# A two-layer decoder trunk on one core: staging slots and a PSUM sum for the first two modulation vectors

## The chip, the cores and the metric

One Trainium2 chip, of which the kernel uses one core. The metric is the device time of one execution in microseconds (us). Three runs of the kernel before gave 2352.1 to 2356.06 us, with a median of 2353.39 us. The engines are called as in the profile: PE (TensorE matmul) and PEld (its weight loads), DVE (VectorE), ACT (ScalarE), POOL (GpSimd), SP (the engine that issues nearly all transfers).

## What is computed

Layer 0 is sparse attention, layer 1 a short gated convolution; each is followed by a SwiGLU FFN. Each of the four sub-layers is normed and modulated by six vectors per layer that come from the condition c. The change touches only the front of layer 0: the first norm and the vectors sh1 (j = 0) and sc1 (j = 1).

```python
c_act = jax.nn.silu(c)                              # c: (1, 1024)
for i in range(2):
    mod = c_act @ ada_w[i] + ada_b[i]               # ada_w: (2, 1024, 6144)
    sh1, sc1, g1, sh2, sc2, g2 = split(mod, 6)      # j = 0 .. 5
    h = _rmsnorm(x, norm1_g[i]) * (1.0 + sc1) + sh1 # x: (1, 1024, 1024)
    y = _dsa_mixer(h, ...) if i == 0 else _short_conv_mixer(h, ...)
    x = x + g1 * y
    h = _rmsnorm(x, norm2_g[i]) * (1.0 + sc2) + sh2
    x = x + g2 * _swiglu(h, ...)
```

All is float32; a large product runs as three products of rounded high and low parts (`hi`, `lo`).

## The kernel before

A planner in the kernel (`Plan`) records every operation with an engine, an estimated cost and a priority (`plan.pri`, smaller is sooner). `drain` then emits the instructions in the order in which its own model of the engines would start them; each engine runs its list strictly in that order. Every instruction therefore carries line 244 (the emitter), and the rows are told apart by their tiles. A change at the front shifts the model's times, so it can also change the order much later.

The front is `Attention.first_norm` (line 851). x arrives as eight tiles `xs` of 128 tokens by 1024 (four in the slot `lo0`, four in `lo1`). PE transposes each in eight 128x128 pieces into two PSUM banks `ps_mm`, ACT copies four pieces at a time to `xt`, and ACT squares the tile with a running sum (`junk`, `ss`). After four tiles a small chain on DVE and ACT (`rst`, with a square root) gives `nr`; PE spreads it over the partitions (`ps_L`), and DVE multiplies it into `zs`, eight tiles of 128x512 for each half of the tokens.

For the modulation vectors the loop `for j in (1, 0)` loads 1024 rows of `ada_w` in eight tiles of 128x1024 (512 KB). Per tile (a step, k = 0 to 7) DVE multiplies columns 0 to 639 by the condition `cact` and adds them to `sc` (`ada_step`, 128x640), and PE multiplies the last 384 columns with `cact` in three matmuls that have one column each (`ada_pe`, 128x1; the profile counts each twice). In the kernel before every step of `ada_pe` takes a `ps_mm` bank, and DVE adds its three columns to `mod` (128x3). At the end PE sums `sc` over the partitions by matmuls with `ones` (`ps_sm`, five of one column), DVE adds this to `mod` (128x5), and for j = 1 `ada_scale` makes `aff`. Slots: odd k take the tile `stage`, k = 0 and 4 the ring `raw` (two slots), k = 2 and 6 the ring `s4` (three).

When `aff` and `mod` of j = 0 are there, DVE and ACT form `nz` (normed and modulated, 128x512, eight for each half), ACT rounds it to `hhi`, DVE takes the rest as `hlo`, and PE begins with the product of 72 columns for the indexer (`ps_mm<-hhi,whi 128*72`), 24 matmuls for each half of the tokens; called the first product here.

`vectors` (line 614) loads the norm gains, convolution weights and small tables as rows, and DVE copies two of them (`COPY C<-S`), before PE transposes all to `vec`. `setup` (line 585) does this for c and the biases, with the Silu that gives `cact`.

Of the kernel before, what the change touches and what calls it, by code (L numbers as in the profile page):

```python
# [9 lines left out]
F32 = mybir.dt.float32  # L10
# [5 lines left out]
ALU = mybir.AluOpType  # L16
# [459 lines left out]
R_C, R_N1, R_N2, R_CW, R_G, R_IF = 0, 8, 24, 40, (64, 96), 66  # L476
# [10 lines left out]
class Trunk:  # L487
# [94 lines left out]
        nc.vector.tensor_tensor(out, r, t, op=ALU.mult)  # L582


    def setup(self, c, ada_b, arenas):
        nc, cp = self.nc, self.cp
        self.ident = ident = cp.tile([P, P], F32, name="ident")
        nc.gpsimd.memset(ident, 1.0)
        nc.gpsimd.affine_select(ident, ident, pattern=[[-1, P]], compare_op=ALU.is_equal,
                                fill=0.0, base=0, channel_multiplier=1)  # L590
        self.ones = cp.tile([P, 1], F32, name="ones")
        nc.vector.memset(self.ones, 1.0)
        self.blk4 = cp.tile([P, 4], F32, name="blk4")
        nc.vector.memset(self.blk4, 0.0)
        for i in range(4):
            nc.vector.memset(self.blk4[32 * i:32 * i + 32, i:i + 1], 1.0)
        rc, rowb = arenas[0].part_of(0)[0:8, P:2 * P], arenas[1].part_of(0)[0:96, 0:P]
        nc.sync.dma_start(rc, c.rearrange("o (k p) -> (o k) p", p=P))
        self.plan.pri = 1.2
        nc.sync.dma_start(rowb, ada_b.rearrange("l (k p) -> (l k) p", p=P))  # L600
        self.cact = cp.tile([P, 8], F32, name="cact")
        pv = self.ps("sm")
        nc.tensor.transpose(pv[:, 0:8], rc, ident[:8, :8])
        nc.scalar.activation(self.cact, pv[:, 0:8], AF.Silu)
        self.adab = cp.tile([P, 96], F32, name="adab")
        pb = self.ps("sm")
        nc.tensor.transpose(pb[:, 0:96], rowb, ident[:96, :96])
        nc.vector.tensor_copy(self.adab, pb[:, 0:96])
        mod = cp.tile([P, 2, 6, 8], F32, name="mod")
        self.mod = [[mod.part_of((i, j))[:, i, j] for j in range(6)] for i in range(2)]  # L610
        aff = cp.tile([P, 2, 2, 8], F32, name="aff")
        self.aff = [[aff.part_of((i, j))[:, i, j] for j in range(2)] for i in range(2)]

    def vectors(self, n1, n2, conv_w, gq, gk, lg, lb, rope_c, arenas, kgb):

        nc, cp = self.nc, self.cp
        rows = arenas[0].part_of(1)[:, 0:P]
        nc.vector.memset(rows, 0.0)
        for r0, n, v in ((R_N1, 16, n1.rearrange("l (k p) -> (l k) p", p=P)),
                         (R_N2, 16, n2.rearrange("l (k p) -> (l k) p", p=P)),  # L620
                         (R_CW, 24, conv_w.rearrange("o w (k p) -> (o w k) p", p=P)),
                         (R_IF, 1, rope_c)):
            nc.sync.dma_start(rows.part_of((1, r0))[r0:r0 + n, :], v)
        g = arenas[1].part_of(96)[96:98, 0:HD]
        for r, v in enumerate((gq, gk)):
            nc.sync.dma_start(g[r:r + 1], v)
        self.plan.pri = 1.15
        for i, r in enumerate(R_G):
            nc.vector.tensor_copy(
                rows.part_of((1, r))[r:r + 2].rearrange("p (r q) -> p r q", q=32),  # L630
                g[:, 32 * i:32 * i + 32].unsqueeze(1).to_broadcast([2, 4, 32]))
        self.vec = vec = cp.tile([P, P], F32, name="vec")
        pv = self.ps("sm")
        rd = [1] + [(1, r) for r in (R_N1, R_N2, R_CW, R_IF, *R_G)]
        nc.tensor.transpose(pv[:, 0:P], rows.part_of(rd), self.ident)
        nc.vector.tensor_copy(vec, pv[:, 0:P])
        self.plan.pri = 25.5
# [31 lines left out]
        if j in (1, 4) and c0 + n == KT or layer == 0 and j == 1:  # L669
            self.ada_scale(layer, j)  # L670

    def ada_pe(self, w, layer, j, k, d0, tag="mm"):


        n = w.free // P
        ps, dst, b0 = self.ps(tag), self.mod[layer][j][:, d0:d0 + n], layer * 48 + j * 8 + d0
        for d in range(n):
            self.nc.tensor.matmul(ps[:, d:d + 1], w[:, blk(d)], self.cact[:, k:k + 1],
                                  start=True, stop=True)
        self.nc.vector.tensor_tensor(dst, ps[:, 0:n], dst if k else self.adab[:, b0:b0 + n],  # L680
                                     op=ALU.add)

    def ada_scale(self, layer, j):

        n, r0 = (0, R_N1) if j == 1 else (1, R_N2)
        r0 += 8 * layer
        self.nc.vector.scalar_tensor_tensor(self.aff[layer][n], self.mod[layer][j], 1.0,
                                            self.vec[:, r0:r0 + 8], op0=ALU.add, op1=ALU.mult)
# [79 lines left out]
def trunk_kernel(tc, x, c, positions, ada_w, ada_b, norm1_g, norm2_g, attn_w_in, attn_q_norm_g,  # L768
                 attn_k_norm_g, idx_k_ln_g, idx_k_ln_b, attn_w_out, conv_w_in, conv_w,
                 conv_w_out, ffn_w_gate, ffn_w_up, ffn_w_down, rope_c, out):  # L770
    plan = Plan(tc.nc, tc)
    with ExitStack() as ctx:
        ctx.enter_context(tc.manual_schedule())
        tk = Trunk(plan)
        for p in (tk.cp, tk.pp):
# [32 lines left out]
class Attention:  # L808
# [42 lines left out]
    def first_norm(self, x, positions, setup, vectors):  # L851
        tk, nc, plan, sp = self.tk, self.nc, self.plan, self.pj
# [8 lines left out]
        for tt in range(TB):  # L861
# [40 lines left out]
        for half in range(NH):
            z, tags = [], ("rt", "t2", "sw", "rt", "t2", "sw", "rt", "rt")
            for d in range(KT):
# [3 lines left out]
                a, b = tk.aff[0][0][:, d:d + 1], tk.mod[0][0][:, d:d + 1]  # L908
# [929 lines left out]
```

## Time and profile before

| | before |
|---|---|
| median of three runs | 2353.39 us |
| the profiled execution's own time | 2353.95 us |
| its span | 2352.2 us |
| PE busy | 2263.6 us (96%) |
| DVE busy | 1887.3 us (80%) |
| ACT busy | 1121.7 us (48%) |
| DMA, mean over the span | 132 GB/s |

The profiled execution's time is its span and 1.75 us around it, and it lies 0.56 us above the median. Busy times are shares of the whole span; the change is made in its first 75 us, so the stretch itself has to be read. Digits in the slices are tenths; `PEclk` is the clock that PE was granted, in tenths of 2.4 GHz.

### The profile page before, as it was taken

Reading aid. Unit: us, or ns where it says so; the run is one execution under the profiler, and the core shown is the slowest. Engines: PE = TensorE matmul, PEld = TensorE weight load, DVE = VectorE, ACT = ScalarE, POOL = GpSimd, SP = SyncE. Lnnn points to the kernel's source line nnn. Section 1 sums busy time; section 2 is a strip of 40 time slices with the busy share of each in tenths; the row PEclk is TensorE's granted clock in tenths of the full one; section 3 lists DMA queues with packets and bytes.
Section 4 is the critical chain, followed back from the end, with each engine's and each line's share of the span. In section 5 each row is a group of like instructions: output and inputs, shape, how many; then the busy total and the mean of one; then the engine's idle time right before and its main releaser. Section 6 shows DMA issues by size and latency. Waiting matters only on the chain.

```text
span 2352.2 us, 32869 instructions
## 1 busy us (share of the span) xinstructions
PE 2263.6 (96%) x11743; PEld 1828.6 (78%) x11743; DVE 1887.3 (80%) x3858; ACT 1121.7 (48%) x2106; POOL 5.1 (0%) x19
## 2 busy tenths in 40 slices
PE   7999989999999999999999899999999999999999
PEld 6757866776797778888887677788878888888877
DVE  5789979686589888887699989886898766665996
ACT  4468989857754233333343552223553333333434
POOL 0000000000000000000000000000000000000000
PEclk7999999999999999999999999999999999999999
DMA  7414332322244756443944143334344222238343
GB/s 287 123 53 99 102 105 73 117 91 64 81 140 131 223 177 188 151 153 111 326 139 147 63 131 113 103 90 152 109 126 152 89 90 76 90 119 311 126 161 112
DMA packets 304078, 311.27 MB, mean 132 GB/s; under 512 B 15113, under 2 KB 208682, under 8 KB 303914
## 3 DMA queue, kind: packets, MB, share of 16 engines
q1 hardware_dynamic: 302474, 307.86, 41.1%
q8 instruction: 92, 1.51, 0.3%
q10 hardware_dynamic: 1440, 1.31, 0.2%
q14 instruction: 72, 0.59, 0.1%
HBM read 258.00 MB, written 51.12 MB: 131 GB/s over the span
## 4 chain that ended last, share of the span: by engine, by line
PE 74%; DVE 16%; DMA 6%; ACT 2%; issue 2%; SPq 0%; ACTq 0%; DVEq 0%
PE ps_g L244 38%; PE ps_mm L244 26%; PE ps_sm L244 5%; DVE u L244 2%; PE ps_L L244 2%; PE ps_o L244 2%; DVE wlo L244 2%; DVE sc L244 2%; DMA adaw<-in_ada_w_dram 2%; DVE v L244 2%; DVE s L244 2%; DVE xr L244 1%; ACT p L244 1%; DVE p L244 1%; DVE adacc L244 1%
## 5 line engine op out<-in xcount | busy, mean ns | idle before, releaser
L244 ACT CAST whi<-s 128x512 fp32r<-128x512 f32 x341 | 211.4, 621 | 457.9 <-PE ps_g L244 181.4
L244 PE MATMUL ps_g<-t,whi 128*128 128x512 f32 x1160 | 361.2, 392 | 3.8 <-ACT t L244 2.9
L244 ACT CAST whi<-raw 128x512 fp32r<-128x512 f32 (+1 forms) x271 | 165.9, 618 | 366.2 <-PE ps_g L244 145.5
L244 PE MATMUL ps_g<-h,whi 128*128 128x512 f32 x1080 | 333.9, 390 | 0.0
L244 DVE TENSOR_TENSOR wlo<-raw,whi 128x512 fp32r<-128x512 f32 (+1 forms) x288 | 195.8, 684 | 79.4 <-ACT whi L244 79.0
L244 PEld LDWEIGHTS ps_g<-t,whi 128*128 128x128 f32 x1160 | 218.3, 189 | 51.0 <-ACT t L244 3.3
L244 DVE TENSOR_TENSOR wlo<-s,whi 128x512 fp32r<-128x512 f32 x342 | 232.5, 684 | 26.4 <-ACT whi L244 25.8
L244 PEld LDWEIGHTS ps_g<-h,whi 128*128 128x128 f32 x1080 | 202.2, 188 | 41.6
L244 PE MATMUL ps_g<-t,wlo 128*128 128x512 f32 x580 | 227.6, 392 | 4.8 <-DVE wlo L244 4.7
L244 PE MATMUL ps_g<-ph,whi 128*128 128x512 f32 x660 | 207.6, 393 | 4.4 <-DVE ph L244 2.3
L244 PE MATMUL ps_g<-h,wlo 128*128 128x512 f32 x540 | 210.5, 390 | 0.0
L244 PE MATMUL ps_mm<-t,whi 128*128 128x512 f32 x632 | 198.9, 396 | 4.0 <-ACT whi L244 4.0
L244 PEld LDWEIGHTS ps_g<-ph,whi 128*128 128x128 f32 x660 | 125.3, 190 | 32.4 <-DVE ph L244 3.3
L244 PEld LDWEIGHTS ps_mm<-t,whi 128*128 128x128 f32 x632 | 120.8, 192 | 30.3 <-ACT whi L244 5.1
L244 PEld LDWEIGHTS ps_g<-t,wlo 128*128 128x128 f32 x580 | 109.4, 189 | 29.7 <-DVE wlo L244 7.1
L244 DVE CUSTOM_DVE_ANT_0 p<-ps_L,bias 128x512 f32<-128x512 f32 (+3 forms) x192 | 100.1, 551 | 38.9 <-PE ps_L L244 22.2
L244 PE MATMUL ps_g<-ph,wlo 128*128 128x512 f32 x330 | 130.5, 395 | 0.0
L244 PE MATMUL ps_mm<-t,wlo 128*128 128x512 f32 x316 | 125.3, 396 | 4.7 <-DVE wlo L244 4.6
L244 ACT ACTIVATE junk<-sc,bs 128x896 bf16<-128x896 f32 (+3 forms) x124 | 123.4, 995 | 8.4 <-DVE bs L244 6.6
L244 ACT ACTIVATE p<-p,nm,qsc 128x256 f32<-128x256 f32 (+7 forms) x128 | 113.2, 886 | 21.4 <-DVE nm L244 19.9
L244 DVE SCALAR_TENSOR_TENSOR adacc<-adaw,cact,adacc 128x512 f32<-128x512 f32 x140 | 104.4, 746 | 20.5 <-DMA adaw<-in_ada_w_dram 20.3
L244 PEld LDWEIGHTS ps_g<-h,wlo 128*128 128x128 f32 x540 | 101.4, 188 | 21.6 <-DVE wlo L244 0.4
(331 smaller groups left out, 4713.1 us busy)
## 6 DMA issues: line engine op xcount, KB each, us to landing
ph<-in_ffn_w_down_dram SPq DMA_DIRECT2D x88, 512.0 KB
adaw<-in_ada_w_dram SPq DMA_DIRECT2D x160, 256.0 KB
raw<-in_ffn_w_gate_dram SPq DMA_DIRECT2D x52, 512.0 KB
raw<-in_ffn_w_up_dram SPq DMA_DIRECT2D x52, 512.0 KB
rt<-hid SPq DMA_DIRECT2D x64, 256.0 KB
raw<-in_conv_w_in_dram SPq DMA_DIRECT2D x32, 512.0 KB
hid<-u SPq DMA_DIRECT2D x52, 256.0 KB
raw<-in_ffn_w_down_dram SPq DMA_DIRECT2D x44, 256.0 KB
```

The source lines that it names most:

```text
L244: f(*[a.get() if isinstance(a, Ref) else a for a in args], **{k: a.get() if isinstance(a, Ref) else a for k, a in kw.items()})
```

## The change

- j = 0 no longer uses `raw` and `s4`: its eight tiles go to two staging tiles in the slots `lo0` and `lo1`, the slots of the x tiles. j = 1 keeps `hi0`, two `raw` and two `s4`.
- `ada_pe` adds all eight steps of a vector up in one bank, `ps_o`, of which there is one; DVE adds it to `mod` once at the end instead of eight times.
- The gain of the first norm (`norm1_g`) is loaded and transposed with c in `setup` (24 rows instead of 8), with a DVE copy to `n1`, and `ada_scale` takes it from there. `vectors` is called after the loop, with the priority of the rope tables, 28.5.

```diff
@@ setup
-        rc, rowb = arenas[0].part_of(0)[0:8, P:2 * P], arenas[1].part_of(0)[0:96, 0:P]
-        nc.sync.dma_start(rc, c.rearrange("o (k p) -> (o k) p", p=P))
+        rc, rowb = arenas[0].part_of(0)[0:24, P:2 * P], arenas[1].part_of(0)[0:96, 0:P]
+        nc.sync.dma_start(rc[0:8], c.rearrange("o (k p) -> (o k) p", p=P))
+        nc.sync.dma_start(rc[8:24], n1.rearrange("l (k p) -> (l k) p", p=P))
...
-        nc.tensor.transpose(pv[:, 0:8], rc, ident[:8, :8])
+        nc.tensor.transpose(pv[:, 0:24], rc, ident[:24, :24])
         nc.scalar.activation(self.cact, pv[:, 0:8], AF.Silu)
+        nc.vector.tensor_copy(self.n1, pv[:, 8:24])
@@ ada_pe
-    def ada_pe(self, w, layer, j, k, d0, tag="mm"):
+    def ada_pe(self, w, k, ps):
         n = w.free // P
-        ps, dst, b0 = self.ps(tag), self.mod[layer][j][:, d0:d0 + n], layer * 48 + j * 8 + d0
         for d in range(n):
             self.nc.tensor.matmul(ps[:, d:d + 1], w[:, blk(d)], self.cact[:, k:k + 1],
-                                  start=True, stop=True)
-        self.nc.vector.tensor_tensor(dst, ps[:, 0:n], dst if k else self.adab[:, b0:b0 + n],
-                                     op=ALU.add)
+                                  start=k + d == 0, stop=k == KT - 1 and d == n - 1)
@@ first_norm
-        plan.pri = 13.5
-        vectors((self.C, self.S))
         for j in (1, 0):
             acc = self.score[5 + j][:, 0:5 * P]
-            stage = self.hp.tile([P, 4, D], F32, name="stage%d" % j, tag="hi0" if j else "lo0")
+            stage = [self.hp.tile([P, 4, D], F32, name="stage%d" % j, tag=tag)
+                     for tag in (("hi0",) if j else ("lo0", "lo1"))]
+            ps = tk.ps("o")
             for k in range(KT):
                 plan.pri = 10.0 + k + 8 * (1 - j)
-                if k % 2:
-                    w = stage.part_of(k)[:, k // 2]
+                if j == 0 or k % 2:
+                    w = stage[k // 4 if j == 0 else 0].part_of(k)[:, k % 4 if j == 0 else k // 2]
                 else:
                     w = self.s4() if k % 4 else tk.raw()
                 last = nc.sync.dma_start(w, tk.ada_rows(self.ada_w, 0, j, k))
                 plan.pri = 1.1
                 tk.ada_step(w[:, 0:5 * P], k, acc)
-                tk.ada_pe(w[:, 5 * P:], 0, j, k, 5)
+                tk.ada_pe(w[:, 5 * P:], k, ps)
+            nc.vector.tensor_tensor(tk.mod[0][j][:, 5:], ps[:, 0:3],
+                                    tk.adab[:, 8 * j + 5:8 * j + 8], op=ALU.add)
             tk.ada_end(0, j, [acc])
         plan.pri = 28.5
+        vectors((self.C, self.S))
```

The change also moves instructions. On ACT, at the start of the program, stands before (`junk` is the square of an x tile, `rst` the square root):

```order
L244 ACT_TABLE_LOAD
L244 ACTIVATE cact<-ps_sm 128x8
L244 ACTIVATE junk_197,ss<-xs 128x1024
L244 COPY xt<-ps_mm 128x4x128
L244 ACTIVATE junk_197,ss<-xs 128x1024
L244 COPY xt<-ps_mm 128x4x128 x2
```

and with the change:

```order
L244 ACT_TABLE_LOAD
L244 ACTIVATE junk_198,ss<-xs 128x1024
L244 COPY xt<-ps_mm 128x4x128
L244 ACTIVATE junk_198,ss<-xs 128x1024
L244 COPY xt<-ps_mm 128x4x128 x2
L244 ACT_TABLE_LOAD
L244 ACTIVATE cact<-ps_sm 128x8
```

The Silu moved behind two x tiles, and it has a table load of its own, so that the program has ten of them in place of nine.

On PE, the stretch from the spreading of `nr` to the end of j = 1 stands before (`sc_194` is the sum of j = 1, the steps read `raw`, `stage` and `s`):

```order
L244 MATMUL ps_L<-ident,nr 128x128 x4
L244 MATMUL ps_mm<-ident,xs 128x128 x28
L244 MATMUL ps_mm<-cact,raw 128x1 x3
L244 MATMUL ps_mm<-cact,stage_212 128x1 x3
L244 MATMUL ps_mm<-cact,s_198 128x1 x3
L244 MATMUL ps_mm<-cact,stage_212 128x1 x3
L244 MATMUL ps_sm<-ident,C 128x128
```

and with the change:

```order
L244 MATMUL ps_L<-ident,nr 128x128 x4
L244 MATMUL ps_o<-cact,raw 128x1 x3
L244 MATMUL ps_o<-cact,stage_213 128x1 x3
L244 MATMUL ps_mm<-ident,xs 128x128 x2
L244 MATMUL ps_o<-cact,s_199 128x1 x3
L244 MATMUL ps_mm<-ident,xs 128x128 x6
L244 MATMUL ps_o<-cact,stage_213 128x1 x3
L244 MATMUL ps_mm<-ident,xs 128x128 x7
L244 MATMUL ps_o<-cact,raw 128x1 x3
L244 MATMUL ps_mm<-ident,xs 128x128 x5
```

The last 28 transposes of x, which ran before the first step, now stand between the steps; the last of them stands ahead of the last step of j = 1. The transpose of `C` to `vec` left this place: it now stands inside the first product, 14 of whose matmuls are ahead of it.

On DVE, the end of j = 0 with the change (`sc_194` is now the sum of j = 0, `zs_210` the second half of the tokens):

```order
L244 TENSOR_TENSOR zs_210<-xt,ps_L 128x512
L244 SCALAR_TENSOR_TENSOR sc_194<-stage_445,cact,sc_194 128x640
L244 TENSOR_TENSOR mod<-ps_o,adab 128x3
L244 TENSOR_TENSOR zs_210<-xt,ps_L 128x512 x5
L244 TENSOR_TENSOR mod<-ps_sm,adab 128x5
L244 TENSOR_TENSOR zs_210<-xt,ps_L 128x512
L244 TENSOR_TENSOR wlo<-raw,whi 128x288 x2
L244 TENSOR_SCALAR nz<-zs_186,aff,mod 128x512 x3
L244 TENSOR_TENSOR hlo_493<-nz,hhi_455 128x512 x5
L244 TENSOR_SCALAR nz<-zs_186,aff,mod 128x512 x2
L244 COPY C<-S 2x128
L244 TENSOR_TENSOR hlo_493<-nz,hhi_455 128x512 x3
```

Before, four of the `zs` stood between the last two additions to `mod` and none behind them, and the two copies `C<-S` stood among the products of j = 1. Later in the program the order on PE is nearly that of before until the second block of queries of the attention; from there it differs in many places of the attention and of the first FFN.

## Rows read from the trace of the kernel before

**Rows 1.** The page's parts 1 and 2: busy time of PE and the two PE rows of the 40 slices (58.8 us each).

```profile
PE 2263.6 (96%) x11743; PEld 1828.6 (78%) x11743; DVE 1887.3 (80%) x3858; ACT 1121.7 (48%) x2106; POOL 5.1 (0%) x19
...
PE   7999989999999999999999899999999999999999
...
PEclk7999999999999999999999999999999999999999
```

**Rows 2.** Busy time by stretches of 4 us (span's start in us; then the stretch's length; busy us and count of PE, PEld, DVE, ACT, POOL; granted clock as a share of 2.4 GHz; DMA share; GB/s).

```profile
16.00:20.00 4.00, 2.65 (x12) 2.65 (x13) 1.92 (x7) 3.99 (x9) 0.00 (x0) 0.63 1.00 370
...
24.00:28.00 4.00, 2.70 (x21) 2.22 (x20) 3.71 (x6) 1.66 (x3) 0.00 (x0) 0.91 0.93 312
...
32.00:36.00 4.00, 4.00 (x21) 4.00 (x21) 1.42 (x9) 0.00 (x0) 0.00 (x0) 0.50 0.74 258
...
44.00:48.00 4.00, 4.00 (x21) 4.00 (x20) 2.27 (x6) 0.76 (x2) 0.00 (x0) 0.50 0.03 10
...
68.00:72.00 4.00, 4.00 (x12) 2.16 (x12) 3.71 (x7) 3.97 (x8) 0.00 (x0) 0.57 0.04 15
```

**Rows 3.** Instructions in order of time on ACT, 0 to 30 us (start us, length us, engine, line, operation, output and input, count; in brackets the idle time before and what ended it).

```profile
0.80 1.28 ACT L244 ACT_TABLE_LOAD   x1 [0.80 <-PEq L1825]
2.61 0.18 ACT L244 ACTIVATE cact<-ps_sm 128x8 f32<-128x8 f32 x1 [0.53 <-PE ps_sm L244]
...
12.66 1.06 ACT L244 ACTIVATE junk<-xs 128x1024 bf16<-128x1024 f32 x1
...
13.71 1.06 ACT L244 COPY xt<-ps_mm 128x512 f32<-128x512 f32 x2
14.79 1.28 ACT L244 ACT_TABLE_LOAD   x1
```

**Rows 4.** The same on PE, 14 to 32 us, like rows merged.

```profile
17.35 2.08 PE L244 MATMUL ps_L<-ident,nr 128*128 128x128 f32 x8 [1.86 <-DVE nr L244]
19.22 1.66 PE L244 MATMUL ps_mm<-ident,xs 128*128 128x128 f32 x8
22.08 1.14 PE L244 MATMUL ps_mm<-ident,xs 128*128 128x128 f32 x8 [1.20 <-ACT xt L244]
...
25.23 0.83 PE L244 MATMUL ps_mm<-cact,raw 128*128 128x1 f32 x6
26.07 0.83 PE L244 MATMUL ps_mm<-cact,stage 128*128 128x1 f32 x6
29.31 1.44 PE L244 MATMUL ps_mm<-cact,s 128*128 128x1 f32 x6 [2.41 <-DVE mod L244]
```

**Rows 5.** The same on PE, 36 to 58 us.

```profile
35.84 1.42 PE L244 MATMUL ps_mm<-cact,stage 128*128 128x1 f32 x6
37.12 2.27 PE L244 MATMUL ps_sm<-ones,sc 128*128 128x1 f32 x10
39.25 0.57 PE L244 MATMUL ps_mm<-cact,stage 128*128 128x1 f32 x2
...
41.81 1.63 PE L244 MATMUL ps_L<-ident,nr 128*128 128x128 f32 x6
...
52.06 2.29 PE L244 MATMUL ps_sm<-ones,sc 128*128 128x1 f32 x10 [0.72 <-DVE sc L244]
```

**Rows 6.** The same on DVE, 14 to 34 us.

```profile
17.13 0.16 DVE L244 TENSOR_TENSOR nr<-rst 128x4 f32<-128x4 f32 x1
...
20.66 0.88 DVE L244 SCALAR_TENSOR_TENSOR sc<-stage,cact,sc 128x640 f32<-128x640 f32 x1
...
22.06 0.88 DVE L244 SCALAR_TENSOR_TENSOR sc<-s,cact,sc 128x640 f32<-128x640 f32 x1
...
29.29 0.22 DVE L244 COPY C<-S 2x128 f32<-2x128 f32 x1
...
32.38 0.29 DVE L244 COPY vec<-ps_sm 128x128 f32<-128x128 f32 x1 [0.16 <-PE ps_sm L244]
```

**Rows 7.** The same on DVE, 50 to 58 us.

```profile
51.99 2.47 DVE L244 TENSOR_TENSOR zs<-xt,ps_L 128x512 f32<-128x512 f32 x4
54.39 0.17 DVE L244 TENSOR_TENSOR mod<-ps_sm,adab 128x5 f32<-128x5 f32 x1
```

**Rows 8.** The same on DVE, 71 to 79 us.

```profile
71.46 1.29 DVE L244 TENSOR_TENSOR hlo<-nz,hhi 128x512 fp32r<-128x512 f32 x2 [0.29 <-ACT hhi L244]
```

**Rows 9.** The same on PE, 60 to 76 us: the wait ahead of its second half, and the end of the first product.

```profile
67.81 0.45 PE L244 MATMUL ps_mm<-hlo,whi 128*72 128x512 f32 x1 [0.71 <-DVE hlo L244]
...
69.65 0.63 PE L244 MATMUL ps_mm<-hhi,whi 128*72 128x512 f32 x1
70.08 0.63 PE L244 MATMUL ps_mm<-hlo,whi 128*72 128x512 f32 x1
...
74.28 0.39 PE L244 MATMUL ps_mm<-hlo,whi 128*72 128x512 f32 x1
74.51 0.39 PE L244 MATMUL ps_mm<-hhi,wlo 128*72 128x512 f32 x1
```

**Rows 10.** The issues of transfers by SP, 0 to 62 us.

```profile
33.45 0.33 SPq L244 DMA_DIRECT2D raw<-in_ada_w_dram  x1
```

**Rows 11.** Busy time in two longer stretches (columns as in Rows 2).

```profile
300.00:540.00 240.00, 221.27 (x1911) 167.94 (x1909) 190.00 (x650) 188.78 (x450) 0.00 (x0) 0.98 0.33 102
76.00:120.00 44.00, 43.50 (x252) 37.36 (x251) 28.83 (x63) 13.60 (x25) 0.00 (x0) 1.00 0.43 125
```

More of the change, by code (lines that the diff above doesn't have):

```diff
@@ L582, in rsqrt_small, with setup @@
         nc.vector.tensor_tensor(out, r, t, op=ALU.mult)
-    def setup(self, c, ada_b, arenas):
+    def setup(self, c, ada_b, n1, arenas):
         nc, cp = self.nc, self.cp
@@ L601, in setup @@
         self.cact = cp.tile([P, 8], F32, name="cact")
+        self.n1 = cp.tile([P, 16], F32, name="n1")
         pv = self.ps("sm")
-        nc.tensor.transpose(pv[:, 0:8], rc, ident[:8, :8])
+        nc.tensor.transpose(pv[:, 0:24], rc, ident[:24, :24])
         nc.scalar.activation(self.cact, pv[:, 0:8], AF.Silu)
+        nc.vector.tensor_copy(self.n1, pv[:, 8:24])
         self.adab = cp.tile([P, 96], F32, name="adab")
@@ L612, in setup, with vectors @@
         self.aff = [[aff.part_of((i, j))[:, i, j] for j in range(2)] for i in range(2)]
-    def vectors(self, n1, n2, conv_w, gq, gk, lg, lb, rope_c, arenas, kgb):
+    def vectors(self, n2, conv_w, gq, gk, lg, lb, rope_c, arenas, kgb):
         nc, cp = self.nc, self.cp
@@ L618, in vectors @@
         nc.vector.memset(rows, 0.0)
-        for r0, n, v in ((R_N1, 16, n1.rearrange("l (k p) -> (l k) p", p=P)),
-                         (R_N2, 16, n2.rearrange("l (k p) -> (l k) p", p=P)),
+        for r0, n, v in ((R_N2, 16, n2.rearrange("l (k p) -> (l k) p", p=P)),
                          (R_CW, 24, conv_w.rearrange("o w (k p) -> (o w k) p", p=P)),
@@ L626, in vectors @@
             nc.sync.dma_start(g[r:r + 1], v)
-        self.plan.pri = 1.15
         for i, r in enumerate(R_G):
@@ L633, in vectors @@
         pv = self.ps("sm")
-        rd = [1] + [(1, r) for r in (R_N1, R_N2, R_CW, R_IF, *R_G)]
+        rd = [1] + [(1, r) for r in (R_N2, R_CW, R_IF, *R_G)]
         nc.tensor.transpose(pv[:, 0:P], rows.part_of(rd), self.ident)
         nc.vector.tensor_copy(vec, pv[:, 0:P])
-        self.plan.pri = 25.5
         self.kgb = kgb.rearrange("p (a d) -> p a d", d=HD)
@@ L670, in ada_end @@
             self.ada_scale(layer, j)
-    def ada_pe(self, w, layer, j, k, d0, tag="mm"):
+    def ada_pe(self, w, k, ps):
         n = w.free // P
-        ps, dst, b0 = self.ps(tag), self.mod[layer][j][:, d0:d0 + n], layer * 48 + j * 8 + d0
         for d in range(n):
             self.nc.tensor.matmul(ps[:, d:d + 1], w[:, blk(d)], self.cact[:, k:k + 1],
-                                  start=True, stop=True)
-        self.nc.vector.tensor_tensor(dst, ps[:, 0:n], dst if k else self.adab[:, b0:b0 + n],
-                                     op=ALU.add)
+                                  start=k + d == 0, stop=k == KT - 1 and d == n - 1)
     def ada_scale(self, layer, j):
[L685 to L688, printed above, removed]
+        g = self.n1 if j == 1 else self.vec[:, R_N2:R_N2 + 16]
+        self.nc.vector.scalar_tensor_tensor(self.aff[layer][j == 4], self.mod[layer][j], 1.0,
+                                            g[:, 8 * layer:8 * layer + 8],
+                                            op0=ALU.add, op1=ALU.mult)
     def raw(self):
@@ L779, in trunk_kernel @@
         a = Attention(tk, attn_w_in[0], attn_w_out[0], ada_w, xspill)
-        a.first_norm(x, positions, lambda v: tk.setup(c, ada_b, v), lambda v: tk.vectors(
-            norm1_g, norm2_g, conv_w, attn_q_norm_g, attn_k_norm_g, idx_k_ln_g, idx_k_ln_b,
+        a.first_norm(x, positions, lambda v: tk.setup(c, ada_b, norm1_g, v), lambda v: tk.vectors(
+            norm2_g, conv_w, attn_q_norm_g, attn_k_norm_g, idx_k_ln_g, idx_k_ln_b,
             rope_c, v, a.score[2][:, 256:384]))
```

## The prediction

> **What bounds the kernel now.** I read the page first, then the stretches of time, then each engine's instructions in order. PE is busy 96% of the span, and after the first slice its clock is full in every one [rows 1]; between 76 and 120 us it works 43.50 of 44 us at full clock [rows 11]. So the change, which ends with the first product, is worth what it moves the end of that product: 74.51 us plus a pitch of 0.23 us, 74.74 us [rows 9]. A microsecond gained there stays gained as long as PE stays the bound.
>
> In that front PE is the bound in another way: it has almost no work in it, but at a slow clock. From 32 to 36 and from 44 to 48 us it is busy in all of 4.00 us and is granted 0.50, which is 1.2 GHz [rows 2]. What fills it are the one-column matmuls of the modulation. A step of three starts every 0.84 us at 2.4 GHz (25.23 to 26.07) [rows 4] and every 1.28 us at 1.2 GHz (35.84 to 37.12) [rows 5]. j = 1 is through on PE at 37.12 us, and the last addition to `mod` starts at 54.39 us [rows 5, 7]; from there DVE works without much rest until the last `hlo`, at 71.46 + 1.29 = 72.75 us [rows 8].
>
> **The change, part by part.**
>
> *What goes.* Fourteen of the sixteen small additions to `mod` on DVE, and with them the ping-pong: PE waited 2.41 us for such an addition, since both `ps_mm` banks were full [rows 4]. A load of j = 0 waited for its `raw` slot until 33.45 us [rows 10]. I book neither on its own: what they are worth depends on what PE and DVE do then, and that is worked out below.
>
> *ACT.* The first table load, at 0.80 us, and the Silu of 0.18 us ran while ACT waited for x. With the change the Silu stands behind two x tiles with a load of its own: 1.28 + 0.18 = 1.46 us in a stretch in which the squares and copies follow each other (12.66, 13.71, 14.79) [rows 3]. The chain to `nr` hangs on these, so `ps_L` starts at 17.35 + 1.46 = 18.81 us [rows 4]. Ends: 0, if some of it falls into a wait, and 2.7, if PE also waits for the added row load as long as its 1.20 us at 22.08 [rows 4]. I take 1.46, since ACT has no gap there.
>
> *PE, j = 1.* Before, the 28 last transposes ran ahead of the first step; now they stand between the steps. What PE must do from 18.81 us to the end of j = 1 at 1.2 GHz: `ps_L` 1.87 (17.35 to 19.22), 28 transposes at 1.66 / 8 = 0.208, 5.8, and eight steps at 1.28, 10.2. That ends at 36.7 us. At 2.4 GHz the transposes take 1.14 / 8 = 0.143, 4.0, and the steps 6.7, together with `ps_L` to 31.4 us [rows 4, 5]. Which clock? The mean from 16 to 20 us is 0.63, after PE had waited 1.86 us for `nr` [rows 2, 4]. It came back in an unbroken run of transposes; it fell again after two kinds of steps and the 2.41 us wait. After that no stretch of steps is at 2.4 GHz, although eight products of 128 columns stand among them at 41.81 us [rows 2, 4, 5]. With the change the wait for `nr` is 1.46 us longer, and one-column steps come right behind `ps_L`. I take 1.2 GHz, with a little of the start at the full clock: 36.0 us. Before it was 37.12, so 1.1 us gained.
>
> *PE and DVE, j = 0.* `ps_o` is one bank, so the first step of j = 0 waits until DVE has added j = 1 (0.17 [rows 7]): 36.2 us. Behind that addition on DVE stand the products of j = 0; DVE, which is through with j = 1 at 20.66 + 1.46 + 6 x 1.40 + 0.88 = 31.4 us [rows 6], stands still until then. PE does six steps (7.7), one group of `ones` (39.25 - 37.12 = 2.13) and eight matmuls of the second `ps_L` (1.63 / 6 x 8 = 2.2) [rows 5] before the bank for `zs` is full: 48.2 us. DVE then has two `zs` (2.47 / 4 = 0.62 each) and two products (1.40 - 0.62 = 0.8 each) to the last product [rows 6, 7]: 51.1 us. PE sums `sc` until 53.2, but on DVE five `zs` stand ahead of the addition: 51.1 + 0.1 + 3.1 = 54.3 us. Before: 54.39. The gain of j = 1 is given back, since `zs` that ran in DVE's idle time now wait for PE.
>
> *The loads* for steps 4 to 7 of j = 0 need `lo1`, the slot of the last four x tiles, which is free when the last transpose is done, one step before the end of j = 1, at about 34.7 us. At the 370 GB/s of 16 to 20 us [rows 2] 512 KB take 1.4 us, so the first is there by about 38 and the last by 43 us. PE reads the first at 36.2 + 5.1 + 2.1 = 43.4 us. Hidden, with 5 us to spare; without that cover each us late would be one us.
>
> *DVE to the end.* From the last addition to the last `hlo` it took 72.75 - 54.39 = 18.4 us [rows 7, 8]. New in it are one `zs` (0.62), two copies of 0.22 and the copy of `vec`, 0.29 [rows 6]: 1.35. The wait of 0.29 [rows 8] can go. 54.3 + 19.4 = 73.7 us. PE then has two matmuls of 0.23 left. Before it ended 2.0 us after the last `hlo`, because its clock was 0.57 from 68 to 72 us [rows 2]. Ends 0.5 and 2.0; I take 0.6, as PE waits for each `hlo` and has no arrears: 74.3 us.
>
> *The sum.* 74.3 against 74.74: 0.4 us less. Against the profiled execution's 2353.95 us that is 2353.55; that execution lies 0.56 us above the median of the runs, so the median should be 2353.39 - 0.4 = **2353.0 us**.
>
> *The rest of the program* has the same work in another order from the second block of queries. From 300 to 540 us PE is idle for 240 - 221.27 = 18.73 us [rows 11]. The order could take away or add some of that; no row says which. I take nothing, and a quarter, 4.7 us, as the end on both sides.
>
> **The rivals.** A measurement of this kernel can tell 0.2%, 4.7 us, from no change.
>
> *Faster, the clock holds through j = 1.* If the transposes between the steps keep PE at 2.4 GHz, j = 1 ends at 31.4 us on PE and on DVE, and everything behind moves by 36.0 - 31.4 = 4.6 us: 2353.0 - 4.6 = 2348.4 us. For it: from 24 to 28 us, with transposes and two steps, the mean is still 0.91. Against: it fell right after [rows 2, 4].
>
> *Faster, the clock holds through both.* Then DVE bounds j = 0: eight products (6.4), eight `zs` (5.0) and 1.4 of small work from 31.5 us, 44.3 us instead of 54.3: 2343.0 us. Against: PE was busy in all 4.00 us at 0.50, so it isn't short waits that hold the clock down [rows 2]. The Trainium skill, "TensorE: Matmul & The Clock Gate", section on psum-queue depth-cycling, says that a kernel that goes through PSUM banks in every iteration idles so often between groups that the clock falls; by that rule the single bank would keep it up, and this rival would be the result. The trace doesn't bear it out here, since there is no idle between the steps from 32 to 48 us.
>
> *Slower: the transpose of `vec` inside the first product.* It waits for two copies that stand on DVE behind eight `hlo`, and the rest of the first half's matmuls, ten, wait behind it on PE; then PE waits again for the second half's first `hlo`, as at 67.81 us. After that one wait the clock was 0.57 from 68 to 72 us [rows 2, 9]. With two waits ten and 24 matmuls could run at a pitch of 0.43 (69.65 to 70.08) instead of 0.23 (74.28 to 74.51) [rows 9]: 34 x 0.20 = 6.8 us, of which some 1.3 hide behind the `hlo`. 74.3 + 5.5 = 79.8: 2358.5 us. It decides if PE idles over 2 us more between the halves than before. Against: before, one wait cost the clock once, and in the new order DVE delivers the `hlo` for steps 0 to 4 sooner.
>
> *The rest decides.* The attention's new order costs or gives more than 4.7 us.
>
> **How the numbers follow.** The forecast has 0.60: in it 0.36 within 0.2%, 0.14 faster and 0.10 slower, by the ends of the rest. The clock through j = 1 has 0.16 (0.11 faster, 0.05 within), through both 0.05 (faster), the transpose of `vec` 0.11 (0.09 slower, 0.02 within), the rest alone 0.08 (half and half). Faster 0.34, same 0.43, slower 0.23. The range takes in both faster rivals, 2343, and the slower one with half of the rest's end, 2361.
>
> **What would show it.** Right: a granted clock of 0.5 from about 21 us; the last step of j = 1 at about 36 us; the addition `mod<-ps_sm` of j = 0 at about 54; the first product's end at about 74 us; the same pace of PE up to 300 us. Wrong: steps at a pitch of 0.84 us beyond 24 us; a wait of PE of over 2 us ahead of `ps_sm<-ident,C`; PE idle from 300 to 540 us other than 18.7 by over 4.7.

## The result and the profile after

Four runs of the changed kernel gave 2382.34 to 2387.14 us, median 2385.87; beside them four runs of the kernel before gave a median of 2353.11. The ratio is 1.0135 [1.0117, 1.0152]: **32.8 us slower**, where 0.4 us less was forecast and 2361 us was the upper end.

The page's busy times, as in [rows 1]; span 2383.9 us, the profiled execution's own time 2385.59:

```profile
PE 2287.1 (96%) x11743; PEld 1838.1 (77%) x11743; DVE 1888.9 (79%) x3847; ACT 1123.1 (47%) x2105; POOL 5.1 (0%) x19
```

PE has the same 11743 matmuls as before and is busy 23.5 us longer, though the change gives it nothing new to do. The front came out close to the forecast. On PE in order of time, to hold against [rows 4, 5, 9]:

```profile
18.56 2.08 PE L244 MATMUL ps_L<-ident,nr 128*128 128x128 f32 x8 [1.18 <-DVE nr L244]
...
33.34 1.28 PE L244 MATMUL ps_o<-cact,s 128*128 128x1 f32 x6
...
34.72 1.28 PE L244 MATMUL ps_o<-cact,stage 128*128 128x1 f32 x6
...
74.05 0.39 PE L244 MATMUL ps_mm<-hhi,wlo 128*72 128x512 f32 x1
74.28 0.28 PE L244 MATMUL ps_mm<-hhi,whi 128*128 128x256 f32 x1
```

The steps last 1.28 us, the last of j = 1 ends at 36.00, and the first product gives way to the next one at 74.28. The two additions on DVE, against [rows 7]:

```profile
36.04 0.16 DVE L244 TENSOR_TENSOR mod<-ps_o,adab 128x3 f32<-128x3 f32 x1 [4.92 <-PE ps_o L244]
...
54.03 0.15 DVE L244 TENSOR_TENSOR mod<-ps_sm,adab 128x5 f32<-128x5 f32 x1
```

So nothing was lost by 74 us. To see where it was, each matmul is matched by its tiles and its ordinal with the same matmul before. The lag is its start in a kernel's trace less its start in the trace before, as a median over 40 us (e1 to e8 are experiments of the next section). In e8 nine matmuls of the next product stand inside the first one, and its -2.9 is counted with them as done:

| us | after the change | front shifted back (e1) | before, shifted (e2) | before, 64 B more (e3) | order, scratch, addresses undone (e7) | also `vectors` back (e8) |
|---|---|---|---|---|---|---|
| end of the first product | -0.5 | -0.5 | -1.9 | -2.3 | -3.0 | -2.9 |
| 300 | 5.6 | 4.7 | -1.2 | 2.1 | -1.5 | 1.3 |
| 650 | 23.0 | 5.3 | 18.3 | 1.1 | -3.1 | 0.5 |
| 900 | 22.6 | 7.4 | 15.5 | 1.9 | 1.4 | 3.2 |
| 2320 | 31.6 | 16.7 | 15.0 | 12.3 | 1.0 | 2.9 |

The first column has three separate losses: 6 us between 74 and 300 us, 17 in the attention between 300 and 650, and 9 from 900 us to the end (from 1760 to 2100 us it grows by 0.4 per 40 us). Each has its rows.

**74 to 92 us.** Stretches of 2 us after the change (columns as in [rows 2]):

```profile
80.00:82.00 2.00, 0.93 (x7) 0.61 (x6) 0.00 (x0) 0.00 (x0) 0.00 (x0) 1.00 1.07 280
82.00:84.00 2.00, 0.60 (x6) 0.56 (x7) 0.55 (x2) 0.00 (x0) 0.00 (x0) 1.00 0.12 31
84.00:86.00 2.00, 2.00 (x11) 1.26 (x10) 1.90 (x5) 0.37 (x1) 0.00 (x0) 0.62 0.82 241
86.00:88.00 2.00, 2.00 (x15) 1.84 (x15) 1.15 (x4) 0.00 (x0) 0.00 (x0) 0.50 0.03 9
```

PE has 1.5 us of work in 4 us, and is then granted 0.62 and 0.50 (1.2 GHz). What came late is the rope tables, which go through memory (`rd`) and back to `S`. ACT's queue after the change, and DVE's copy behind it:

```profile
79.27 0.34 ACTq L244 DMA_DIRECT2D rd<-sc  x1
...
82.79 1.76 ACTq L244 DMA_DIRECT2D S<-rd  x4
```

```profile
82.89 0.46 DVE L244 COPY sc<-ps_o 128x288 f32<-128x288 f32 x1 [4.11 <-DMA rd<-sc]
```

and ACT's queue before:

```profile
78.48 0.34 ACTq L244 DMA_DIRECT2D rd<-sc  x1
80.43 1.76 ACTq L244 DMA_DIRECT2D S<-rd  x4
```

The way through `rd` took 82.79 - 79.27 = 3.52 us instead of 1.95: the write is issued 1.45 us behind a weight load to `raw` (2.40 us before), and the DMA share is 1.07 in its stretch. DVE's copy waited 3.0 us for `rd` before and 4.1 after, and PE waited for that copy 0.5 us before and 2.5 after. From 76 to 120 us PE works 41.45 us at a mean clock of 0.92, against 43.50 at 1.00 [rows 11].

**300 to 540 us.** PE is idle for 240 - 210.43 = 29.57 us instead of 18.73 [rows 11], and ACT is busy 6.1 us less; the largest hole runs from 406 to 415.6 us:

```profile
300.00:540.00 240.00, 210.43 (x1779) 160.55 (x1778) 182.54 (x628) 182.70 (x439) 0.00 (x0) 0.94 0.29 89
...
400.00:410.00 10.00, 4.66 (x53) 3.57 (x50) 9.31 (x23) 6.39 (x16) 0.00 (x0) 0.94 0.43 127
410.00:420.00 10.00, 3.72 (x13) 2.07 (x15) 10.00 (x34) 4.29 (x8) 0.00 (x0) 0.50 0.18 56
```

The same two stretches before:

```profile
400.00:410.00 10.00, 8.63 (x90) 6.39 (x89) 10.00 (x29) 7.11 (x17) 0.00 (x0) 1.00 0.17 52
410.00:420.00 10.00, 9.92 (x86) 8.45 (x86) 8.79 (x29) 7.02 (x16) 0.00 (x0) 1.00 0.41 115
```

In the hole PE waits for DVE's work on `mx` (after, PE):

```profile
404.92 1.09 PE L244 MATMUL ps_o<-pf,vst 128*64 128x128 f32 x16 [1.35 <-ACT pf L244]
...
415.64 2.50 PE L244 MATMUL ps_L<-karena,qst 64*128 64x512 f32 x8 [9.62 <-DVE mx L244]
```

Over the whole stretch PE's waits for `mx` come to 10.9 us before and 19.4 after (the sum, the number of waits, the longest):

```profile
PE ps_L L244 <- DVE mx L244: 10.9, 7, 5.7
```

```profile
PE ps_L L244 <- DVE mx L244: 19.4, 7, 9.6
```

DVE is busy throughout the hole (10.00 of 10.00 from 410 us) and does the work in another order: it writes the `bias` of block 4, the fifth block of queries (640 columns), at 413.41 us after the change,

```profile
413.41 0.83 DVE L244 SCALAR_TENSOR_TENSOR bias<-s,s 128x640 bf16<-128x640 f32 x1
```

and at 395.13 before:

```profile
395.13 0.82 DVE L244 SCALAR_TENSOR_TENSOR bias<-s,s 128x640 bf16<-128x640 f32 x1
```

ACT makes passes of the blocks' selection (`junk<-sc,bs`). From 320 to 380 us it ran 7 of them instead of 13, and 3 of block 4 instead of 6. That this is what held the `bias` up is read from the order and not shown: e12 below has the same wait with 5 passes of block 4 in that time, as many as e1, which hasn't the wait. What the traces with the wait share is that the `bias` of block 4 comes 10 to 20 us later than before (after, e2, e4, e12). Matched as a sequence, PE's order from 101 to 334 us is that of before; from 334 to about 865 us 765 matmuls stand elsewhere.

**The rest.** Runs of back-to-back matmuls of 512 columns, before and then after. What counts is the pitch, the time from one start to the next:

```profile
1822.30 0.62 PE L244 MATMUL ps_mm<-h,whi 128*128 128x512 f32 x2
...
1826.38 0.62 PE L244 MATMUL ps_g<-t,whi 128*128 128x512 f32 x2
```

```profile
1822.16 0.62 PE L244 MATMUL ps_mm<-t,whi 128*128 128x512 f32 x2
...
1826.28 0.62 PE L244 MATMUL ps_g<-t,whi 128*128 128x512 f32 x2
```

There are 18 matmuls from the one start to the other: 4.08 / 18 = 226.7 ns before, 4.12 / 18 = 228.9 after, with a full clock and no wait in either. Over a whole trace the mean of `ps_g<-t,whi` is 226.9 and 228.7 ns.

### The profile page after: what moved, and what is told of

It is laid out like the page before. It is cut to its first block, busy times and chain, and to the rows that moved or that the text cites. A ratio compares the mean times of both kernels' runs of the same rounds, so it can differ in the third digit from the quotient of the medians.

```text
span 2383.9 us, 32842 instructions
## 1 busy us (share of the span) xinstructions
PE 2287.1 (96%) x11743; PEld 1838.1 (77%) x11743; DVE 1888.9 (79%) x3847; ACT 1123.1 (47%) x2105; POOL 5.1 (0%) x19
## 4 chain that ended last, share of the span: by engine, by line
PE 57%; DVE 6%; DMA 2%; issue 1%; ACT 0%; SPq 0%; ACTq 0%; DVEq 0%
PE ps_g L244 39%; PE ps_mm L244 15%; PE ps_sm L244 3%; DVE u L244 1%; DVE v L244 1%; DVE xr L244 1%; DVE wlo L244 1%; DMA raw<-in_conv_w_in_dram 1%; DVE s L244 0%; ACT whi L244 0%; DVE adacc L244 0%; DVE t L244 0%; DMA raw<-in_ffn_w_gate_dram 0%; DMA adaw<-in_ada_w_dram 0%; DVE h L244 0%
## 5 line engine op out<-in xcount | busy, mean ns | idle before, releaser
L244 PEld LDWEIGHTS ps_g<-h,wlo 128*128 128x128 f32 x540 | 101.4, 188 | 22.9 <-DVE wlo L244 0.3
```

Of the source, the lines that this page charges most:

```text
L244: f(*[a.get() if isinstance(a, Ref) else a for a in args], **{k: a.get() if isinstance(a, Ref) else a for k, a in kw.items()})
```

## Experiments

**e1 and e2: is it the attention's order?** The planner keeps a model of PE's clock along its planned time, in stretches that begin at `plan.window`. The change makes the planned front 0.354 us shorter. e1 moves the stretches of the changed kernel back by that, behind the first `drain`; e2 moves those of the kernel before the other way.

```diff
+        plan.window -= 0.354        # e1, on the changed kernel
+        plan.window += 0.354        # e2, on the kernel before
```

> The changed kernel; the only edit is one line after the planner has laid out the projection: its clock window is moved back by 0.354 us. By the order listing, PE, DVE, ACT and SP then do from some 90 us to the end, instruction for instruction, what they do in the kernel before; the front is the change's. Theory (the attention's order is what costs): PE's lag behind the kernel before, 5.6 us at 300 us and 23.0 at 650 us, stays at 5.6 through the attention, so 17.4 us go: 2385.9 - 17.4 = 2368.5 us, and the stall of 9.6 us at 406 us is gone. Rival (the order is only different, the time is lost to something else, slower matmuls or loads): 2385.9 within 3, and the stall or another like it stays.

> The kernel before; the only edit is the same line with the opposite sign: the planner's clock window is moved forward by 0.354 us after the projection. By the order listing the attention and all behind it then stand as in the changed kernel, the front as before. Theory (the attention's order costs, and it comes from the planner's clock alone): 2353.1 + 17.4 = 2370.5 us, with an idle time of PE of some 10 us between 395 and 420 us. Rival (the loss needs the changed front): 2353.1 within 3.

e1: 2370.53 us (2368.74 to 2371.75), 15.3 less than the changed kernel. e2: 2369.42 (2361.68 to 2372.55), 16.8 more than before. In e1 PE's order from 101.4 to 1200 us is that of before, matmul for matmul; in e2 765 of the 6400 matmuls of that stretch stand elsewhere, from 334 us on, as after the change. The hole is gone in e1,

```profile
400.00:410.00 10.00, 9.79 (x96) 7.04 (x94) 10.00 (x39) 8.04 (x19) 0.00 (x0) 1.00 0.19 55
410.00:420.00 10.00, 8.62 (x79) 7.65 (x78) 9.82 (x29) 5.76 (x13) 0.00 (x0) 1.00 0.23 62
```

and there in e2, whose front has the instructions of before (PE):

```profile
409.93 2.51 PE L244 MATMUL ps_L<-karena,qst 64*128 64x512 f32 x8 [9.62 <-DVE mx L244]
```

So the order is worth 15 to 17 us, and no instruction has to be added or taken away for it.

**e3 and e4: is it the new tile's address?** `n1` has 16 floats, 64 bytes of each partition, and stands in the pool ahead of nearly everything. e3 puts 64 bytes there in the kernel before; e4 makes it 128 in the changed one.

```diff
+        cp.tile([P, 16], F32, name="gap")                          # e3
-        self.n1 = cp.tile([P, 16], F32, name="n1")                 # e4
+        self.n1 = cp.tile([P, 32], F32, name="n1")[:, 0:16]
```

> The kernel before with one unused tile of 64 bytes per partition in the pool const, where the change puts n1: every tile on the left side of SBUF moves up by 64 bytes, as in the changed kernel, and no instruction moves. Theory (the address of the moving operand sets the pitch of the matmuls): the pitch of the 512-column products of the gate, up and down stages goes from 227 to 228.6-229.7 ns, as in the changed kernel, and the end moves by the 9.2 us by which the lag grows there from 650 us to the end: 2362.3 us. Rival (the pitch follows the order of the work, or what runs beside it): 2353.1 within 1.5, pitch 227.

> The changed kernel, n1 in a tile of 128 bytes per partition instead of 64, its second half unused: no instruction moves, and the left side of SBUF lies 128 bytes above where it lay before instead of 64. Theory (the address modulo 128 sets the pitch): pitch back to 227 ns, 2385.9 - 9.2 = 2376.7 us. Rival (any move of the addresses costs, or none does): 2385.9 within 1.5.

e3: 2366.05 (2363.19 to 2367.23), +13.5 against its own before (2352.59). Its pitch is 229.8 ns and its lag grows by 0.4 per 40 us from 1760 to 2100 us, as after the change; 10.4 us come between 900 and 2320 us. In all it is 3.7 more than expected: its way through `rd` also took 3.53 us, and a lead of 2.3 us at the end of the first product is a lag of 1.9 at 90 us. e4 missed: 2399.24, 13.4 more than the changed kernel, where less was expected. PE in the same place as above:

```profile
1821.87 0.63 PE L244 MATMUL ps_g<-h,whi 128*128 128x512 f32 x2
...
1826.07 0.63 PE L244 MATMUL ps_mm<-t,whi 128*128 128x512 f32 x2
```

4.20 / 18 = 233.3 ns. So addresses count, but not by a multiple of 128 bytes.

**e5: the pitch by itself.** 96 groups of 48 matmuls of 512 columns and nothing else (nothing of the reference is computed): the moving operand at 32 offsets in steps of 32 bytes (letters), the weights at three (`wx`, `wy` 64 and `wz` 256 bytes higher). Mod 256 the weights of `wx` and `wz` lie at 224 and those of `wy` at 32; moving `md` lies at 224, and each letter 32 further.

> A kernel of its own that computes nothing of the reference: 96 groups of 48 matmuls (128x128 weights, 512 columns, fp32r, back to back, weights reloaded for each) while the other engines rest. The moving operand starts at 32 addresses 32 bytes apart (ma at 128 modulo 512), the weights at 480, 32 and 224 modulo 512 (wx, wy, wz). In the large kernels the pitch was 227 ns with the moving tile at 480, 229 at 32, 232.6 at 96, the weights at 480 in all three. Theory 1 (the address of the moving operand sets it): the pitch changes with the group's letter in the same way in wx, wy and wz. Theory 2 (its distance from the weights): the pattern moves by two letters from wx to wy and by eight to wz. Rival (only with other engines' traffic beside it): one pitch for all 96 groups.

PE, one row a group; the next start less a row's own, over 48, is the pitch:

```profile
40.66 11.05 PE L45 MATMUL wx_md<-move,weight 128*128 128x512 f32 x48
51.55 11.37 PE L45 MATMUL wx_me<-move,weight 128*128 128x512 f32 x48
62.75 11.16 PE L45 MATMUL wx_mf<-move,weight 128*128 128x512 f32 x48
73.75 11.37 PE L45 MATMUL wx_mg<-move,weight 128*128 128x512 f32 x48
...
419.57 11.07 PE L45 MATMUL wy_mf<-move,weight 128*128 128x512 f32 x48
430.48 11.37 PE L45 MATMUL wy_mg<-move,weight 128*128 128x512 f32 x48
441.68 11.16 PE L45 MATMUL wy_mh<-move,weight 128*128 128x512 f32 x48
452.68 11.37 PE L45 MATMUL wy_mi<-move,weight 128*128 128x512 f32 x48
...
753.69 11.07 PE L45 MATMUL wz_md<-move,weight 128*128 128x512 f32 x48
764.60 11.37 PE L45 MATMUL wz_me<-move,weight 128*128 128x512 f32 x48
```

`wx_md`, at distance 0 from the weights: 10.89 / 48 = 226.9 ns. `wx_me`, 32 further: 11.20 / 48 = 233.3. `wx_mf`, 64 further: 11.00 / 48 = 229.2. With weights 64 higher the fast letter is `mf` (10.91), two letters on; with weights 256 higher it is `md` again (10.91). At the other distances in steps of 32 bytes the pitch is 233.1 to 234.1. So the distance between the two operands counts, mod 256 bytes, and the kernels fit: 226.9 before, 228.7 and 229.8 with 64 bytes (after, e3), 232.8 with 128 (e4).

**e6: the wait for the tables.** Both it and e7 keep e1's line. The rope tables use two of the `score` tiles as scratch, in the order 4, 3, and the copy that waited 4.11 us needs one of them. e6 turns the order round.

```diff
-        tk.rope_tables(positions, self.C, self.S, self.score[4:2:-1], self.rd)
+        tk.rope_tables(positions, self.C, self.S, self.score[3:5], self.rd)
```

> e1_after_window with one more edit: the rope tables take their scratch tiles in the other order (score[3:5] for score[4:2:-1]), so that the tile which the DMA to rd reads is no longer the one into which DVE copies the first product's transposes. By the order listing nothing moves behind 90 us. Theory (the stall of PE at 80 us comes from that DMA): DVE's wait of 4.11 us goes, PE's lag of 4.7 us at 120 us falls to -0.4, 2370.5 - 5.1 = 2365.4 us. Rival (the stall comes from the tables' own time, which DVE and ACT now reach later, and the next step waits for S in any case): the lag stays at 4 or more, 2370.5 within 1.5.

A miss: 2369.27 (2367.93 to 2371.84), which can't be told from e1. The copy no longer waits, but DVE and PE now wait for the table itself, which took 4.79 us through `rd` (DVE's wait with its sum, count and longest, then PE's row):

```profile
DVE sw L244 <- DMA S<-rd: 4.3, 1, 4.3
```

```profile
84.02 1.06 PE L244 MATMUL ps_o<-ident,S 32*128 32x32 f32 x8 [2.20 <-DMA S<-rd]
```

**e7: the address undone in the changed kernel.** `n1` lives in the columns of `vec` that are its own anyway, so no tile is added (`vec` is only allocated earlier); the planner's shift becomes 0.379.

```diff
-        self.n1 = cp.tile([P, 16], F32, name="n1")
+        self.vec = cp.tile([P, P], F32, name="vec")
+        self.n1 = self.vec.part_of(1)[:, R_N1:R_N2]
...
-        nc.vector.tensor_copy(vec, pv[:, 0:P])
+        nc.vector.tensor_copy(self.vec.part_of(2)[:, R_N2:], pv[:, R_N2:P])
```

> e6_scratch with one more edit: n1 lies in the columns of vec that were kept for it, so no tile on the left side of SBUF has another address than in the kernel before (the planner's window is moved by 0.379 us for the same order behind). Theory (order, scratch and addresses are all there is): what is left of the change is the front, whose first product ended 0.46 us earlier, so 2352.6 - 0.4 = 2352.2 us, pitch 227 ns in the gate, up and down stages. Rival (a fourth cause): more than 2355.

2358.96 (2354.65 to 2361.22, 12 runs): 10.3 less than e6, with a pitch of 226.9 ns and no growth of the lag from 1760 to 2100 us. Missed by 6.8: it is still slower than before, 1.0021 [1.0013, 1.003].

**e8: `vectors` where it was.** e7 with the call back ahead of the loop, at its old priorities (two lines inside `vectors` that set them are left out here), and a planner's shift of 0.792.

```diff
+        plan.pri = 13.5
+        vectors((self.C, self.S))      # ahead of the loop over j
...
-        vectors((self.C, self.S))      # behind it
```

> e7_three_undone with one more edit: the small vectors are loaded and transposed where they were in the kernel before, ahead of the modulations; the slots of the staging and the sum in one PSUM bank stay (planner's window 0.792 us, same order behind 100 us as in the kernel before). Theory (the vectors' and tables' late start is what is left: in e6 and e7 the DMA of the second table to rd, issued 1.1 us behind the second weight load, took 4.8 and 3.6 us where it took 2.0 in the kernel before, and PE waited for S): the table's DMA goes out ahead of that weight load, PE's lag at 120 us is at most -0.4, 2359.0 - 6 = 2353 or less. Rival (what is left of e7 lies behind 700 us, where its profiled run lost 4 us between 720 and 850): 2359 within 1.5, with the lag rising there again.

2355.27 (2351.34 to 2359.21, 11 runs), by medians 3.7 less than e7, and 1.0015 [1.0006, 1.0024] of before; that interval overlaps e7's, so the gain is hardly resolved. The tables go out ahead of the weight load (79.51 - 77.76 = 1.75 us through `rd`, ACT's queue),

```profile
77.76 0.34 ACTq L244 DMA_DIRECT2D rd<-sc  x1
79.51 1.76 ACTq L244 DMA_DIRECT2D S<-rd  x4
```

and at the end of the first product PE is 2.9 us ahead of before. But of those 2.9 nothing is left at 90 us (a lag of 0.6): the work behind it wasn't there yet (PE),

```profile
74.70 0.39 PE L244 MATMUL ps_mm<-hhi,whi 128*128 128x256 f32 x1 [1.28 <-ACT whi L244]
...
82.93 0.68 PE L244 MATMUL ps_o<-ident,S 32*128 32x32 f32 x8 [0.83 <-DMA S<-rd]
```

since ACT, which rounds that `whi`, had waited for a small transfer:

```profile
74.03 1.14 ACT L244 CAST whi<-raw 128x512 fp32r<-128x512 f32 x2 [2.60 <-DMA C<-rd]
```

**e9 and e10: a gap of 64 bytes for the first layer's input.** Before, `hhi` lies 64 bytes off its weights. The same line in e8 (e9) and in the kernel before (e10) moves it.

```diff
+        sel.tile([P, 16], F32, name="gap")
```

> e8_vectors_back with an unused tile of 64 bytes per partition in the pool sel: all tiles of the pools h and o move down by 64 bytes, no instruction moves. By e5 the pitch is 227 ns where the moving operand and the weights start at the same address modulo 256, 229 where the moving one is 64 bytes further on, 233 elsewhere; hhi and hlo are 64 bytes further on (pitch 229.6 before). Theory (distance from the weights): pitch of the projection's products 227, some 650 matmuls of 512 columns or their worth by 2.6 ns, 1.7 us less than e8. Rival (only what e5 measured alone): same as e8 within 0.8.

> The kernel before with that tile of 64 bytes in sel and nothing else. Theory: pitch of hhi and hlo from 229.6 to 227 ns and 2353.4 - 1.7 = 2351.7 us. Rival: no change in pitch or time.

The pitch of `ps_mm<-hhi,whi` falls as expected, from 229.7 ns before to 227.1 and 227.4. The time does not, and both missed: 2358.24 (e9, 3.0 more than e8 by medians) and 2355.13 (e10, 1.0008 [1.0, 1.0017]). e10 leads by 1.6 us at 300 us, between e2 (1.2) and e12 (3.8), whose fronts are untouched, and lags by 1.2 at 2320. Whether the shorter pitch arrives there and is lost again, these runs don't tell.

**e11: the tables on another queue.** e8 with the tables' transfers issued by POOL, or by SP, so that ACT waits for none.

```diff
-            nc.scalar.dma_start(dr.rearrange("c f t -> (c f) t"), n)
+            nc.gpsimd.dma_start(dr.rearrange("c f t -> (c f) t"), n)   # or nc.sync; the reads alike
```

> e8_vectors_back with the ten DMAs of the rope tables issued by POOL, which has nothing to do there, in place of ACT. In e8 the first product ended 4.0 us earlier than in the kernel before, and PE was 0.6 us behind it at 86 us: it had waited 1.28 us for a weight cast on ACT, which stood behind the issue of the C loads (ACT waits there until rd has landed), and 0.83 us for S. Theory (what is left of the change's gain is lost to ACT's queue): both waits go, PE is 2 us ahead at 86 us, 2355.3 - 2.7 = 2352.6 us. Rival 1 (the next wait, for S itself or for the loads of raw, ends as late as before): 2355.3 within 1. Rival 2 (the issue on POOL is slower, S comes later): 2357 or more.

> The same with SP in place of POOL: SP's queue then holds a load of raw behind the issue of the C loads. Theory: as e11_tables_pool, 2352.6 us. Rival (a load of raw comes late and PE waits for weights): 2356 or more.

No gain: 2356.71 (1.0011 [1.0, 1.0022]) and 2356.02 (1.0006 [0.9996, 1.0016]). At the end of the first product PE is 4.0 and 2.9 us ahead of before, counted as for e8 (2.9 there too, and not the 4.0 that the expectation has). By POOL both of e8's waits go and PE still leads by 2.4 us at 90 us, as the theory had it; by SP it waits 1.5 us for `S` and lags by 0.5. At 2320 us they lag by 5.4 and 3.9: what POOL keeps is lost further back.

**e12: how small a shift does it?**

```diff
+        plan.window += 0.10          # on the kernel before
```

> The kernel before; the planner's clock window is moved forward by 0.10 us after the projection, where e2 moved it by 0.354. By the order listing the attention comes out in a third order. Theory (the order of the kernel before is one draw of many, and a good one; any shift of the planner's time draws again): the attention's bias of block 4 comes late as in e2, 2353 + 10 to 20 us. Rival (0.354 us is a special value): 2353 within 3.

2368.39 (2366.21 to 2376.21), +14.6: a tenth of a microsecond in the planner's model redraws the attention, with a wait like the two above (PE):

```profile
407.25 2.50 PE L244 MATMUL ps_L<-karena,qst 64*128 64x512 f32 x8 [9.19 <-DVE mx L244]
```

## Why the prediction was wrong

**What held.** Point by point, the head came out as worked: `ps_L` at 18.56 (forecast 18.81), the last step of j = 1 at 36.00 (36.0), the addition of j = 1 at 36.04 (36.2), that of j = 0 at 54.03 (54.3), the first product's end at 74.28 (74.3). The gain of j = 1 was given back on DVE, which stood still for 4.92 us ahead of its addition. The single bank did not hold the clock up: the steps run at 1.28 us, the length that went with a granted clock of 0.50, 1.2 GHz, before [rows 2, 5]. (The trace after has no record of the clock ahead of 64 us, and its column says 1.00 there.) e7, with the same slots and bank, has the record, 0.50 with PE busy almost without a gap:

```profile
24.00:28.00 4.00, 4.00 (x21) 4.00 (x21) 4.00 (x7) 1.12 (x3) 0.00 (x0) 0.50 1.04 412
...
44.00:48.00 4.00, 3.94 (x19) 3.86 (x19) 2.37 (x4) 0.00 (x0) 0.00 (x0) 0.50 0.97 287
```

So both clock rivals fell. The Trainium skill ("TensorE: Matmul & The Clock Gate", the section on psum-queue depth-cycling) says that a kernel that cycles through PSUM banks idles so often between groups that its clock falls. As the prediction applied that to this front the trace doesn't agree: with one bank the clock was 0.50 all the same. No wait of over 2 us came ahead of the transpose of `vec`. That the end met the forecast within 0.1 us is luck in part: the five kernels with the changed front (after, e1, e4, e6, e7) end the first product at 71.7 to 74.3 us. And the digit 9 in [rows 1], read as a full clock, means 0.9 or more; from 300 to 540 us it was 0.98 [rows 11].

**The step that failed** is "*The rest of the program*", where I wrote "I take nothing, and a quarter, 4.7 us, as the end on both sides". The rest was worth 32 us. The prediction's own sign for it came true: PE's idle time from 300 to 540 us was 29.57 us, 10.8 more than before. Two causes are shown by experiments, the third is read from the trace:

- *The order*, 15.3 us by e1 (16.8 by e2 and 14.6 by e12 from the other side). The text had it as a rival, "The rest decides", with a chance of 0.08 and no price. A quarter of PE's idle time was no bound: that share was the idle time of an order that happened to fit. The rows for a better price were there: 10.9 of PE's 18.73 us were waits for `mx`, and DVE is busy 190.00 of 240 us and ACT 188.78 [rows 11], so late work on DVE can cost a wait as long as the 9.62 us above, and then the clock (0.50 from 410 to 420 us).
- *The addresses*, 10.3 us by e7 against e6 (9.0 by the lag after the change from 900 to 2320 us). The text has no term for them, nor for `n1` at all; its 64 bytes moved all tiles that lie behind it. Nothing in the trace before warned of it but one pair of pitches, 229.7 for `hhi` and 226.9 ns for `t`, at the same shape and clock.
- *74 to 92 us*, about 5 us of lag, not shown by an experiment: e6 gave nothing back, and e8's 3.7 us are hardly resolved. "The change, which ends with the first product" and "A microsecond gained there stays gained" both failed. The write through `rd` stood closer behind a weight load, PE waited for DVE's copy and then for `S`, and its clock fell. The place of `vectors` isn't needed for that, since e3, with the front of before, has the slow way through `rd` too. PE is the bound only while its operands are there.

In medians, from 2385.87 back to before: e1 -15.3, e6 -1.3 (not resolved), e7 -10.3, e8 -3.7 (hardly resolved). That leaves 2.2 us over before, with the slots, the single bank and the early row load. At the first product these bring little: the five kernels with the front of before end it at 71.6 to 74.7 us, median 72.5; those with slots and bank and the old place of `vectors` (e8, e9 and both of e11), with the interleaved matmuls taken off, at 70.7 to 73.2, median 71.8. The two ranges overlap. So 74.74, from which my sum started, was the slow end of a spread of 3 us that a single execution doesn't show; a forecast of 0.4 us was finer than that. By 300 us nothing of it is left: the latter lag by -1.0 to 2.3 us, the former by -3.8 to 2.1. Where the last 2 us go is not settled; the runs that lead at 650 us (e7, e10, both of e11) lose 3.4 to 4.6 us by 900. PE is idle there for 10.45 to 13.16 us in these four against 9.67 before, mostly waiting for rounded weights (`wlo`, `whi`); why these come no sooner is open. No version beat the kernel before.

## What to carry to other kernels

An edit ahead of a list scheduler is two edits: first hold the later order fixed (here one line that shifts the planner's model) and then price the edit; give the redrawn order a term of its own, about as large as what small shifts produce (15 to 17 us here, in two redraws of the kernel before), not as the idle time left in the present order. A new tile, however small, moves the addresses of what is allocated behind it, so put it where a tile has columns to spare or behind the operands, and compare the matmul pitch before and after. A gain at the front is kept only if what follows is ready, so find the next wait, its transfer and that transfer's queue before it is booked.

## What the runs showed of the hardware

- The pitch of a 128x512 matmul depends on the distance between the moving operand and the weights within a partition, mod 256 bytes: 226.9 ns at 0, 229.2 at 64, 233.1 to 234.1 at the other distances in steps of 32, at a full clock and without waits (e5). Over the whole program 64 bytes cost some 10 us (e6 to e7, e3).
- The tables' short way through memory, from the issue of the second write to `rd` to the issue of the read, took 1.75 and 1.79 us where the write was issued ahead of the weight load to `raw` (e8, e9), 1.95 to 2.35 where it came 2.4 us behind it (before, e2, e12), 2.50 and 3.53 at 1.9 us (e10, e3), and 3.1 to 4.8 at 1.45 us (after, e1, e4, e6, e7).
- After 4 us with about 1.5 us of work PE was granted 0.62 and then 0.50 in the next two stretches of 2 us, although it was busy in all of them (84 to 88 us after the change).
